# The down projection by products of seven as well, with its activation forms made in gate and up and passed through DRAM

## The chip, the cores and the metric

The kernel runs on one core of a Trainium2 chip. The metric is device time in microseconds (us); of the kernel before, three runs were timed, and the median stands for it. All details come from one more execution, taken by the hardware profiler. Names of engines: PE is the matrix engine (TensorE), DVE is VectorE, ACT is ScalarE, POOL is GpSimd, SP is the engine whose queue issues most transfers.

## The reference, cut to what matters

One block of a streaming encoder, on 512 positions (T) and 2048 channels (D): a norm, an input projection, two mixers, an output projection, and then the part that the change touches, a gated feed-forward net with 5632 inner channels (FF), a residual add and a last norm.

```python
def conv_ffn(h, w_gate, w_up, conv_w, conv_b, w_down):
    L = h.shape[1]
    a = h @ w_gate
    a_pad = jnp.pad(a, ((0, 0), (CONV_WIDTH - 1, 0), (0, 0)))
    a = sum(conv_w[j] * a_pad[:, j:j + L] for j in range(CONV_WIDTH)) + conv_b
    return (jax.nn.silu(a) * (h @ w_up)) @ w_down
...
    x = x + jnp.concatenate([o_a, o_b], axis=-1) @ w_out[l]
    h = rmsnorm(x, norm2_gain[l])
    x = x + conv_ffn(h, w_ffn_gate[l], w_ffn_up[l], ffn_conv_w[l], ffn_conv_b[l], w_ffn_down[l])
return rmsnorm(x, final_norm_gain)
```

Everything is float32. The kernel keeps that precision by splitting each operand of a product into a rounded part (hi) and a rest (lo), and by adding three matmuls: hi by hi, hi by lo, lo by hi.

## The kernel before

The program works on tiles of 128 channels by 512 positions. Stages, in the order of time: input projection, mixers and output projection (0 to 898 us); gate and up (904.7 to 1785.3 us); down (1787.9 to 2290.9 us), whose last rows are already the final norm.

**Gate and up by seven products.** For one row block f (128 of the 5632 inner channels, 44 blocks), gate and up are two outputs, and the positions are two halves of 256: a 2 by 2 block product, done with seven block products in place of eight. `glu(f)` asks for them one by one through `product` (L810). Product number i takes one weight combination, in the order `a11, s2, a12, s3, s1, a22, s4`, and one form of the activations, in the order of `NAMES`: `b11, n2, b21, t3, n1, n4, b22`. A form is a hi and a lo tile of 128 by 256 for each of 8 pairs of input blocks, so a product is 8 x 3 = 24 matmuls of 256 columns (L819 to L821), and a row block 168. `prepare` (L789) runs two products ahead (`LEAD`): ACT makes `fhi` (L807), DVE `flo` (L808) from a weight tile `wq` of 128 by 1024; four of each (pool `wh`) exist at a time. The weights come from DRAM by SP (L763); s1 and s3 are sums that a second, accumulating transfer from POOL makes (L765), s2 and s4 are DVE sums (L783). Eight tiles `wq` exist (pool `wf`). After its products, `glu` forms the gated value `uu` (L838 to L858), splits it into `ah` and `al` (L860, L861) and stores both in DRAM (`actd`, L863).

**Down by plain products.** The 44 blocks stand in four groups of 11 (`GF`, `NG`). For each of 16 output blocks d of 128 channels, one group is 11 x 3 = 33 matmuls of 512 columns, added to the residual tile `x1[d]` (L900). The activations come back from `actd`, issued by POOL (`acts_of`, L886); the weights come in pieces `raw` (L142) and are split by ACT (L149) and DVE (L150). In the last group, 12 output blocks are done like that, and the last four (`late`) with positions on the output's rows: 4 x 33 matmuls (L983 to L985), between which the final norm runs (`norm`, L955 to L975; `gained`, L948, scales 12 blocks by 4 quarters on ACT).

**What sets the order.** A scheduler writes one fixed order for each engine, from its own estimates of times; each engine runs its list in order, and a transfer waits on its queue's engine for its source and for a free target.

Of the kernel before, what the change touches and what calls it, by code (L numbers as in the profile page):

```python
# [8 lines left out]
F32 = mybir.dt.float32  # L9
# [13 lines left out]
GF = 11  # L23
NG = NF // GF
# [12 lines left out]
NPIECE_D = NF * KT * P // PIECE  # L37
QH = T // 2
KP = KT // 2
FORM = KP * P  # L40
LEAD = 2
DMA_SUMS = True
# [11 lines left out]
def tile_hymba_block(ctx: ExitStack, tc: tile.TileContext, xT, wst, wgu, wdn, wfb, consts, out, out_t):  # L54
# [10 lines left out]
    def closed(*names):  # L65
        for name in names:
            pools.pop(name)[0].__exit__(None, None, None)
# [28 lines left out]
    def f32(ap):  # L96
        return ap.bitcast(F32)
# [569 lines left out]
    actd = dr.tile([NF, 2, P, T], F32, name="actd")  # L667
# [18 lines left out]
    forms = {n: [] for n in NAMES}  # L686
    acc2 = tt.tile([P, T], F32, name="acc2")

    def form(name, j, src):
        pool = tt if j < KP - 1 else tl  # L690
        hi = pool.tile([P, QH], F32R, name=f"{name}h{j}")
        lo = pool.tile([P, QH], F32R, name=f"{name}l{j}")
        s.activation(hi, src, AF.Copy)
        v.tensor_tensor(lo, src, f32(hi), op=ALU.subtract)
        forms[name].append((hi, lo))

    def pair_forms(j, ha, hb):
        b11, b12, b21, b22 = ha[:, 0:QH], ha[:, QH:T], hb[:, 0:QH], hb[:, QH:T]

        def temp():  # L700
            return xr.tile([P, QH], F32, name="tq", tag="tq", bufs=2)

        form("b11", j, b11)
# [3 lines left out]
        form("n1", j, n1)  # L707
        form("n2", j, n2)
        form("b21", j, b21)
        v.tensor_tensor(n2, n2, b21, op=ALU.add)  # L710
        form("n4", j, n2)
        t3 = temp()
        v.tensor_tensor(t3, b22, b12, op=ALU.subtract)
        form("t3", j, t3)
        form("b22", j, b22)
# [25 lines left out]
    closed("xr")  # L741
    R2 = cp.tile([P, T], F32, name="R2", tag="R")
    nR2 = tl.tile([P, T], F32, name="nR2")
# [12 lines left out]
    raw = {}  # L756

    def W():
        return wf.tile([P, FORM], F32, name="wq", tag="wq")

    def load(f, name, q, q2=None):
        t = raw[f, name] = W()
        nc.sync.dma_start(out=t, in_=wgu[f, q])  # L763
        if q2 is not None:
            gp.dma_start(out=t, in_=wgu[f, q2], accum_op=ALU.add)  # L765

    def loads(f):

        if DMA_SUMS:
            load(f, "s1", 0, 1)  # L770
            load(f, "a11", 2)
            load(f, "s3", 0, 2)
            load(f, "a12", 3)
            load(f, "a22", 1)
        else:
            load(f, "a21", 0)
            load(f, "a22", 1)
            load(f, "a11", 2)
            load(f, "a12", 3)

    def add(f, name, x, y, into=None):
        t = raw[f, name] = W() if into is None else into
        v.tensor_tensor(t, raw[f, x], raw[f, y], op=ALU.add)  # L783

    def sums(f):
        if not DMA_SUMS:
            add(f, "s1", "a21", "a22")
            add(f, "s3", "a21", "a11", raw[f, "a21"])
        add(f, "s2", "s1", "a11")  # L789

    ready = {}

    def prepare(g):
        f, i = divmod(g, 7)
        if f >= NF:
            return
        if i == 0:
            sums(f)
            if f + 1 < NF:
                loads(f + 1)  # L800
        name = ORDER[i]
        if name == "s2":
            add(f, "s4", "s2", "a12")
        t = raw.pop((f, name))
        hi = wh.tile([P, FORM], F32R, name="fhi", tag="fhi")
        lo = wh.tile([P, FORM], F32R, name="flo", tag="flo")
        s.activation(hi, t, AF.Copy)  # L807
        v.tensor_tensor(lo, t, f32(hi), op=ALU.subtract)  # L808
        ready[g] = (hi, lo)

    def product(g, ps, first=True):
        prepare(g + LEAD)
        hi, lo = ready.pop(g)
        rhs = forms[NAMES[g % 7]]
        for j in range(KP):
            a, b = hi[:, j * P:(j + 1) * P], lo[:, j * P:(j + 1) * P]
            th, tl = rhs[j]
            kw = {"skip_group_check": not first}
            pe.matmul(ps, lhsT=a, rhs=th, start=(first and j == 0), stop=False, **kw)  # L819
            pe.matmul(ps, lhsT=a, rhs=tl, start=False, stop=False, **kw)  # L820
            pe.matmul(ps, lhsT=b, rhs=th, start=False, stop=(j == KP - 1), **kw)  # L821
            step()
# [4 lines left out]
    def G(name, shape=(P, T), dt=F32):  # L827
        return gt.tile(list(shape), dt, name=name, tag=name)

    def glu(f):  # L830
        cw = con[:, C_CW + 3 * f:C_CW + 3 * f + 3]
        g = 7 * f
        L, H = slice(0, QH), slice(QH, T)
        x, y, z, w = half(mm), half(mx), half(mm), half(mx)
        p1, u2, u3 = (G(n, (P, QH)) for n in ("p1", "u2", "u3"))
        a, uu = G("a"), G("uu")
        product(g, x)
        s.activation(p1, x, AF.Copy)  # L838
        product(g + 1, y)
        v.tensor_tensor(u2, p1, y, op=ALU.add)  # L840
        product(g + 2, x, first=False)
        s.activation(a[:, L], x, AF.Copy)
        product(g + 3, y, first=False)
        v.tensor_tensor(u3, p1, y, op=ALU.add)
        product(g + 4, z)
        v.tensor_tensor(uu[:, H], u3, z, op=ALU.add)
        product(g + 5, w)
        v.tensor_tensor(uu[:, L], u3, w, op=ALU.subtract)
        product(g + 6, z, first=False)
# [9 lines left out]
        hi, lo = G("ah", dt=F32R), G("al", dt=F32R)  # L859
        s.activation(hi, uu, AF.Copy)  # L860
        v.tensor_tensor(lo, uu, f32(hi), op=ALU.subtract)  # L861
        for i, part in enumerate((hi, lo)):
            nc.sync.dma_start(out=actd[f, i], in_=f32(part))  # L863

    loads(0)
    for g in range(LEAD):
        prepare(g)
    for f in range(NF):
        glu(f)
    closed("gt", "wh", "wf", "tl", "tt")  # L870


    wr = opened("wr", 3)
    wp = opened("wp", 4)
    pq = opened("pq", 81, "right")
# [5 lines left out]
    A = X = O  # L881

    def acts_of(f):
        parts = (O(F32R), O(F32R))
        for i, part in enumerate(parts):
            gp.dma_start(out=f32(part), in_=actd[f, i])  # L886
        return parts

    acts = [acts_of(f) for f in range(GF)]
    x1 = []  # L890
    for d in range(KT):
        t = X()
        gp.dma_start(out=t, in_=x1d[d])
        x1.append(t)
    for g in range(NG - 1):
        nxt = []
        for d in range(KT):
            ps = MX()
            unit(ps, range(GF), acts)
            v.tensor_tensor(x1[d], x1[d], ps, op=ALU.add)  # L900
            if d < GF:
                nxt.append(acts_of((g + 1) * GF + d))
        acts = nxt
# [22 lines left out]
    for d in range(ND):  # L926
        ps = MX()
        unit(ps, range(GF), acts)
        v.tensor_tensor(x1[d], x1[d], ps, op=ALU.add)
        square_acc(acc3, x1[d], d == 0)  # L930
        if d == ND - 2:
            ws.pool = O
    late = [ws.four() for _ in range(GF)]
    part = sm.tile([P, 4], F32, name="part")

    def sums3():
        yield 5
# [40 lines left out]
    for i in range(4):  # L978
        ys = gained(i)
        ps = MX()  # L980
        for k, (hi, lo) in enumerate(late):
# [3 lines left out]
            pe.matmul(ps, lhsT=xh, rhs=lo, start=False, stop=(k == GF - 1))  # L985
# [3 lines left out]
    closed("pq", "wp", "wr", "dr", "mx", "mm", "sm", "cp")  # L989


def _weights(w_in, w_out, w_gate, w_up, w_down):
# [22 lines left out]
    for g in range(NG):  # L1015
        rows = w_down[g * GF * P:(g + 1) * GF * P]
        nd = KT if g + 1 < NG else ND
        parts += [cols(rows, d * P, P) for d in range(nd)]
        parts += [cols(rows, nd * P, D - nd * P)] if nd < KT else []
# [8 lines left out]
    return rows_of(head), np.ascontiguousarray(wgu.reshape(NF, 4, P, FORM)), rows_of(parts)  # L1028
# [34 lines left out]
```

## Time and profile before

| what | us |
|---|---|
| median of 3 timed runs | 2302.2 |
| lowest and highest | 2300.54, 2302.64 |
| the profiled execution, its own time | 2302.55 |
| its span, first to last instruction | 2300.8 |
| PE busy in the span | 2273.4 |
| DVE, ACT, POOL busy | 1464.9, 939.2, 171.6 |

The times in the rows below count from the start of the span. A row of busy time gives the engine, how long it worked and in how many instructions; a timeline row gives start and duration of an instruction, and in brackets how long its engine had been idle and what ended that. "PEclk" is the granted clock of the PE as a share of full speed.

### The profile page before, as it was taken

To read this page: it belongs to the slowest core of one execution; us is meant where nothing else is said; L and a number is where in the kernel's file an instruction comes from. 1 tells how busy PE (TensorE), PEld (TensorE's weight loads), DVE (VectorE), ACT (ScalarE), POOL (GpSimd) and SP (SyncE) were. 2 spreads that over 40 slices of the span, in tenths; PEclk is the share of its full clock that TensorE was granted. 3 is DMA by queue.
4 is the path that set the end of the run, shared out by engine and by line. 5 is a ranking of instruction groups with operands and counts; after the bars stand their busy time and mean duration, and the time that the engine had idled before them with its cause. 6 is when DMAs were issued, how large, how long until landed. Compare 5 with 4: busy or idle time off the path is not lost.

```text
span 2300.8 us, 34411 instructions
## 1 busy us (share of the span) xinstructions
PE 2273.4 (99%) x13662; PEld 2012.7 (87%) x13662; DVE 1464.9 (64%) x2194; ACT 939.2 (41%) x1484; POOL 171.6 (7%) x259
## 2 busy tenths in 40 slices
PE   8999999999999998999999999999999999999998
PEld 7888888788888887999999999999999788888886
DVE  6666467556457565888888888888887333333345
ACT  5333233334335454544444554454444222222234
POOL 4000000000000000000000000000000512000000
PEclk9999999999999999999999999999999999999999
DMA  5222322222222455877877887878784955223223
GB/s 177 83 83 83 100 74 96 74 83 80 86 83 74 142 163 177 226 212 207 216 215 214 212 212 209 216 200 222 208 217 136 375 198 196 92 97 99 85 100 110
DMA packets 112210, 352.67 MB, mean 153 GB/s; under 512 B 12816, under 2 KB 19088, under 8 KB 112048
## 3 DMA queue, kind: packets, MB, share of 16 engines
q1 hardware_dynamic: 89568, 272.67, 36.0%
q0 software_dynamic: 22336, 77.67, 15.4%
q8 instruction: 107, 1.75, 0.3%
q14 instruction: 55, 0.45, 0.1%
q10 hardware_dynamic: 144, 0.12, 0.0%
HBM read 318.96 MB, written 31.46 MB: 152 GB/s over the span
## 4 chain that ended last, share of the span: by engine, by line
PE 95%; DMA 2%; DVE 1%; issue 1%; ACT 0%; POOL 0%; DVEq 0%; ACTq 0%; POOLq 0%
PE pq L819 12%; PE pq L820 12%; PE pq L821 12%; PE mmt L201 9%; PE mmt L203 9%; PE mmt L202 9%; PE mxt L202 7%; PE mxt L201 7%; PE mxt L203 7%; PE mmt L286 2%; PE mmt L284 2%; PE mmt L285 2%; DMA ot<-actd 1%; DMA wq<-wgu 1%; DMA raw<-wdn 1%
## 5 line engine op out<-in xcount | busy, mean ns | idle before, releaser
L150 DVE TENSOR_TENSOR wlo<-raw,whi 128x512 fp32r<-128x512 f32 x453 | 316.3, 699 | 464.5 <-ACT whi L149 424.9
L149 ACT ACTIVATE whi<-raw 128x512 fp32r<-128x512 f32 x453 | 284.8, 630 | 686.3 <-PE mxt L202 322.2
L807 ACT ACTIVATE fhi<-wq 128x1024 fp32r<-128x1024 f32 x308 | 326.6, 1061 | 365.7 <-PE pq L820 323.0
L808 DVE TENSOR_TENSOR flo<-wq,fhi 128x1024 fp32r<-128x1024 f32 x308 | 376.3, 1222 | 58.2 <-ACT fhi L807 52.4
L201 PE MATMUL mmt<-at,whi 128*128 128x512 f32 x896 | 354.8, 396 | 0.0
L203 PE MATMUL mmt<-at,wlo 128*128 128x512 f32 x896 | 349.8, 390 | 0.0
L202 PE MATMUL mmt<-at,whi 128*128 128x512 f32 x896 | 349.3, 390 | 0.0
L201 PE MATMUL mxt<-ot,whi 128*128 128x512 f32 x660 | 262.2, 399 | 2.9 <-ACT whi L149 2.7
L202 PE MATMUL mxt<-ot,whi 128*128 128x512 f32 x660 | 261.8, 397 | 0.5 <-DMA ot<-actd 0.5
L203 PE MATMUL mxt<-ot,wlo 128*128 128x512 f32 x660 | 261.6, 397 | 0.5 <-DVE wlo L150 0.5
L203 PEld LDWEIGHTS mmt<-at,wlo 128*128 128x128 f32 x896 | 168.2, 188 | 35.9
L201 PEld LDWEIGHTS mmt<-at,whi 128*128 128x128 f32 x896 | 168.3, 188 | 34.9 <-issue 1.9
L202 PEld LDWEIGHTS mmt<-at,whi 128*128 128x128 f32 x896 | 168.4, 188 | 33.1
L201 PEld LDWEIGHTS mxt<-ot,whi 128*128 128x128 f32 x660 | 124.5, 189 | 34.8 <-ACT whi L149 2.9
L202 PEld LDWEIGHTS mxt<-ot,whi 128*128 128x128 f32 x660 | 124.6, 189 | 31.8 <-DMA ot<-actd 2.1
L203 PEld LDWEIGHTS mxt<-ot,wlo 128*128 128x128 f32 x660 | 124.7, 189 | 30.6 <-DVE wlo L150 1.0
L765 POOL DMA_DIRECT2D wq<-wgu x88 | 75.9, 862 | 782.1 <-DVE flo L808 388.1
L783 DVE TENSOR_TENSOR wq<-wq 128x1024 f32<-128x1024 f32 x88 | 107.5, 1222 | 3.5 <-DMA wq<-wgu 2.0
L286 PE MATMUL mmt<-wlo,at 128*128 128x512 f32 x256 | 100.6, 394 | 4.4 <-DVE wlo L150 4.4
L819 PE MATMUL pq<-b11h,fhi 128*128 128x256 f32 x352 | 100.2, 285 | 3.6 <-ACT fhi L807 3.6
L284 PE MATMUL mmt<-whi,at 128*128 128x512 f32 x256 | 101.7, 397 | 0.3 <-ACT whi L149 0.3
L821 PE MATMUL pq<-b11h,flo 128*128 128x256 f32 x352 | 99.9, 284 | 1.3 <-DVE flo L808 1.3
(303 smaller groups left out, 5067.7 us busy)
## 6 DMA issues: line engine op xcount, KB each, us to landing
wq<-wgu SPq DMA_DIRECT2D x220, 512.0 KB, 4.5
raw<-wst SPq DMA_DIRECT2D x143, 512.0 KB, 3.5
wq<-wgu POOLq DMA_DIRECT2D x88, 512.0 KB, 7.3
raw<-wdn SPq DMA_DIRECT2D x87, 512.0 KB, 3.5
ot<-actd POOLq DMA_DIRECT2D x88, 256.0 KB, 6.6
actd<-ah SPq DMA_DIRECT2D x44, 256.0 KB, 3.2
actd<-al SPq DMA_DIRECT2D x44, 256.0 KB, 3.0
xt<-xT SPq DMA_DIRECT2D x16, 256.0 KB, 5.3
```

The source lines that it names most:

```text
L149: s.activation(hi, src, AF.Copy)
L150: v.tensor_tensor(lo, src, f32(hi), op=ALU.subtract)
L201: pe.matmul(ps, lhsT=a, rhs=xh[:, ts], start=(first and i == 0), stop=False)
L202: pe.matmul(ps, lhsT=a, rhs=xl[:, ts], start=False, stop=False)
L203: pe.matmul(ps, lhsT=b, rhs=xh[:, ts], start=False, stop=(last and i == n - 1))
L284: pe.matmul(pss[i], lhsT=xh[:, ts], rhs=hi, start=(k == 0), stop=False)
L286: pe.matmul(pss[i], lhsT=xh[:, ts], rhs=lo, start=False, stop=(k == KT - 1))
L807: s.activation(hi, t, AF.Copy)
L808: v.tensor_tensor(lo, t, f32(hi), op=ALU.subtract)
L819: pe.matmul(ps, lhsT=a, rhs=th, start=(first and j == 0), stop=False, **kw)
L820: pe.matmul(ps, lhsT=a, rhs=tl, start=False, stop=False, **kw)
L821: pe.matmul(ps, lhsT=b, rhs=th, start=False, stop=(j == KP - 1), **kw)
```

## The change

Of the 44 row blocks of the down projection, 40 become 20 pairs, and two output blocks d are done together: again a 2 by 2 block product (two inner blocks by two output blocks, halves of 256 positions) with seven products. Three chunks of 7, 7 and 6 pairs; in each chunk 8 units (two output blocks each); a unit has 7 products of n x 3 matmuls of 256 columns, n being 7 or 6. The other four row blocks (`FL`) stay as they were, with the late blocks and the final norm.

The code of `prepare` and `product` becomes a class `Seven` with one list of units, 44 of gate and up and then 24 of down, so that the weights of the next unit are loaded and split while the last one runs, through one ring of weight tiles (`wf`, now 7 in place of 8). s1 and s3 of a down unit are DVE sums, and s2 and s4 are now both made before the first product of a unit.

The forms of the down projection (seven per pair, hi and lo) are made in `glu` from two values `uu` of neighbouring blocks: four more DVE operations, seven ACT and seven DVE splits of 128 by 256, and 14 stores of 128 KB each per pair into `formd` (DRAM). At the start of a chunk, 98 (84) loads of 128 KB bring them back, on SP, into the tiles that held the forms before (`T7`: 14 tiles a name, one chunk). The residual tiles come in the first chunk, on POOL.

```diff
-    wf = opened("wf", 8)
-    wh = opened("wh", LEAD + 2)
+    wf = opened("wf", 7, "right")
+    wh = opened("wh", LEAD + 2, "right")
...
+    def T7(name):
+        return tt.tile([P, QH], F32R, name=name, tag=name, bufs=BUFS)
...
+            if i == 0:
+                if u == 0:
+                    self.loads(0)
+                if not self.units[u][2]:
+                    self.sum(u, "s1", "a21", "a22")
+                    self.sum(u, "s3", "a21", "a11", into="a21")
+                self.sum(u, "s2", "s1", "a11")
+                self.sum(u, "s4", "s2", "a12")
+                if u + 1 < len(self.units):
+                    self.loads(u + 1)
...
+        if f >= 2 * NPAIR:
+            hi, lo = G("ah", dt=F32R), G("al", dt=F32R)
...
+        def put(name, src):
+            hi, lo = G("of", (P, QH), F32R, bufs=6), G("of", (P, QH), F32R, bufs=6)
+            s.activation(hi, src, AF.Copy)
+            v.tensor_tensor(lo, src, f32(hi), op=ALU.subtract)
+            for i, part in enumerate((hi, lo)):
+                nc.sync.dma_start(out=formd[NAMES.index(name), f // 2, i], in_=f32(part))
+
+        seven(halves(*uus), lambda: G("tq", (P, QH), bufs=2), put)
...
+    for c, n in enumerate(CHUNKS):
+        dforms = {}
+        for i, name in enumerate(NAMES):
+            dforms[name] = []
+            for p in range(at, at + n):
+                parts = (T7(name), T7(name))
+                for k, part in enumerate(parts):
+                    nc.sync.dma_start(out=f32(part), in_=formd[i, p, k])
+                dforms[name].append(parts)
+        at += n
+        for m in range(KP):
+            if c == 0:
+                for d in (2 * m, 2 * m + 1):
+                    x1.append(xp.tile([P, T], F32, name=f"x1_{d}"))
+                    gp.dma_start(out=x1[d], in_=x1d[d])
...
+            sv.product(x, dforms)
+            s.activation(p1, x, AF.Copy)
+            sv.product(y, dforms)
+            v.tensor_tensor(u2, p1, y, op=ALU.add)
+            v.tensor_tensor(xe[:, H], xe[:, H], u2, op=ALU.add)
...
+    closed("gt", "wh", "wf", "tt")
...
-    acts = [acts_of(f) for f in range(GF)]
...
+    for f in range(FL):
+        acts.append((O(F32R), O(F32R)))
+        for i, part in enumerate(acts[-1]):
+            nc.sync.dma_start(out=f32(part), in_=actd[f, i])
...
-    late = [ws.four() for _ in range(GF)]
+    late = [ws.four() for _ in range(FL)]
```

The order on SP's queue where gate and up end and down begins, before: the stores of the last blocks, and the weights `raw` of down.

```order
L863 DMA actd_5863<-ah_18031 128x512
L863 DMA actd_5863<-al_18032 128x512
L142 DMA raw_18346<-wdn 128x512 x2
L142 DMA raw_18357<-wdn 128x1024
L142 DMA raw_18391<-wdn 128x1024
L142 DMA raw_18431<-wdn 128x1024
L863 DMA actd_5863<-ah_18249 128x512
L863 DMA actd_5863<-al_18250 128x512
L142 DMA raw_18471<-wdn 128x1024
```

The same place now: the loads of forms of chunk 0 (28 of 98 stand ahead of this piece, `b11` and `n2`), the last weight load `wq` of the second down unit, and the stores of the last gate and up block; 62 further loads of forms stand behind the last store, and behind them the weights of the third down unit.

```order
L936 DMA b21_19091<-formd_5864 128x256
L792 DMA wq_18953<-wd7 128x896
L936 DMA b21_19092<-formd_5864 128x256
...
L936 DMA b21_19103<-formd_5864 128x256
L904 DMA actd_5863<-ah_19021 128x512
L936 DMA b21_19104<-formd_5864 128x256
L904 DMA actd_5863<-al_19022 128x512
L936 DMA b21_19107<-formd_5864 128x256
```

What moved: the activations, which POOL's queue brought back, are now on SP's queue, in one row with the stores and the weights, each held up by the one ahead.

The order on PE at the first products of down, before: from the last matmul of gate and up straight into the first two output blocks (`mxt_18345`, `mxt_18411`), by activations `ot` and weights `whi`, `wlo`.

```order
L821 MATMUL pq_18039<-b22h7_7565,flo_18163 128x256
L201 MATMUL mxt_18345<-ot_18269,whi_18349 128x512
L202 MATMUL mxt_18345<-ot_18270,whi_18349 128x512
L203 MATMUL mxt_18345<-ot_18269,wlo_18350 128x512
L201 MATMUL mxt_18345<-ot_18273,whi_18349 128x512
L201 MATMUL mxt_18411<-ot_18269,whi_18359 128x512
```

Now, late in the first down unit (output `pq_19237`, its last form `b22`), the second unit (outputs `pq_19445` and `pq_19446`, forms `b21` and `t3`) is woven in.

```order
L850 MATMUL pq_19445<-b21_19112,fhi_19452 128x256
L851 MATMUL pq_19445<-b21_19111,flo_19453 128x256
L849 MATMUL pq_19445<-b21_19115,fhi_19452 128x256
L850 MATMUL pq_19445<-b21_19116,fhi_19452 128x256
L850 MATMUL pq_19237<-b22_19204,fhi_19348 128x256
L851 MATMUL pq_19237<-b22_19203,flo_19349 128x256
L851 MATMUL pq_19445<-b21_19115,flo_19453 128x256
L849 MATMUL pq_19446<-t3_19119,fhi_19478 128x256
L849 MATMUL pq_19237<-b22_19207,fhi_19348 128x256
```

What moved: the plain products are gone from this place, and where the first unit takes its last form, 241 of the two units' 294 matmuls stand ahead of its last one; 53 are left.

The order on DVE inside gate and up, at the start of a unit's weights, before: `flo` is the rest of a weight tile, `al` that of the gated value, and the two sums stand together.

```order
L858 TENSOR_TENSOR uu<-uu,t 128x512
L840 TENSOR_TENSOR u_12730<-p_12729,pq 128x256
L808 TENSOR_TENSOR flo<-wq,fhi 128x1024
L861 TENSOR_TENSOR al<-uu,ah 128x512
L783 TENSOR_TENSOR wq<-wq 128x1024 x2
L808 TENSOR_TENSOR flo<-wq,fhi 128x1024
L844 TENSOR_TENSOR u_12731<-p_12729,pq 128x256
```

The same place now, in every second block (in the other ones it holds three operations of the forms in place of eight): `of` and `tq` belong to the forms of down.

```order
L833 TENSOR_TENSOR flo<-wq,fhi 128x1024
L913 TENSOR_TENSOR of<-tq,of 128x256
L812 TENSOR_TENSOR wq<-wq 128x1024
L913 TENSOR_TENSOR of<-uu,of 128x256
L702 TENSOR_TENSOR tq<-tq,uu 128x256
L833 TENSOR_TENSOR flo<-wq,fhi 128x1024
L913 TENSOR_TENSOR of<-tq,of 128x256
L812 TENSOR_TENSOR wq<-wq 128x1024
L913 TENSOR_TENSOR of<-tq,of 128x256
L884 TENSOR_TENSOR u_13381<-p_13379,pq 128x256
L913 TENSOR_TENSOR of<-uu,of 128x256
```

What moved: the one operation `al` went, and 11 smaller ones per pair of blocks stand between the splits of the weights and the sums.

## Rows read from the trace of the kernel before

**Rows 1.** First part of the page: busy time, share, instructions of each engine.

```profile
PE 2273.4 (99%) x13662; PEld 2012.7 (87%) x13662; DVE 1464.9 (64%) x2194; ACT 939.2 (41%) x1484; POOL 171.6 (7%) x259
```

**Rows 2.** Windows: stretch and length, PE, PEld, DVE, ACT, POOL busy, PEclk, DMA share, GB/s.

```profile
915.00:1767.00 852.00, 852.00 (x7201) 852.00 (x7201) 715.36 (x858) 428.23 (x518) 73.27 (x85) 1.00 0.79 211
1785.00:1788.00 3.00, 0.33 (x4) 0.13 (x2) 1.72 (x3) 1.45 (x3) 2.54 (x5) 1.00 0.95 337
1788.00:1796.00 8.00, 7.49 (x19) 5.18 (x20) 4.60 (x8) 2.71 (x5) 5.43 (x11) 0.57 0.96 312
1796.00:1915.00 119.00, 118.34 (x502) 93.44 (x501) 38.56 (x58) 27.18 (x43) 39.44 (x74) 1.00 0.71 261
```

**Rows 3.** Timeline of DVE in one gate and up block: start, duration, instruction, [idle].

```profile
1379.75 0.41 DVE L844 TENSOR_TENSOR u<-p,pq 128x256 f32<-128x256 f32 x1
1380.15 1.22 DVE L808 TENSOR_TENSOR flo<-wq,fhi 128x1024 fp32r<-128x1024 f32 x1
1382.02 0.42 DVE L846 TENSOR_TENSOR uu<-u,pq 128x256 f32<-128x256 f32 x1 [0.64 <-PE pq L821]
1383.04 1.23 DVE L808 TENSOR_TENSOR flo<-wq,fhi 128x1024 fp32r<-128x1024 f32 x1 [0.60 <-ACT fhi L807]
...
1395.50 0.68 DVE L861 TENSOR_TENSOR al<-uu,ah 128x512 fp32r<-128x512 f32 x1
1396.10 2.48 DVE L783 TENSOR_TENSOR wq<-wq 128x1024 f32<-128x1024 f32 x2
...
1399.63 0.41 DVE L844 TENSOR_TENSOR u<-p,pq 128x256 f32<-128x256 f32 x1
```

**Rows 4.** Timeline of DVE in down, two residual adds, 33 matmuls apart.

```profile
2132.93 0.69 DVE L900 TENSOR_TENSOR ot<-ot,mxt 128x512 f32<-128x512 f32 x1 [1.67 <-PE mxt L203]
...
2140.63 0.69 DVE L900 TENSOR_TENSOR ot<-ot,mxt 128x512 f32<-128x512 f32 x1 [0.98 <-PE mxt L203]
```

**Rows 5.** Issues of transfers on the page: KB each, median us to landing.

```profile
wq<-wgu SPq DMA_DIRECT2D x220, 512.0 KB, 4.5
...
wq<-wgu POOLq DMA_DIRECT2D x88, 512.0 KB, 7.3
raw<-wdn SPq DMA_DIRECT2D x87, 512.0 KB, 3.5
...
actd<-al SPq DMA_DIRECT2D x44, 256.0 KB, 3.0
```

**Rows 6.** Timeline of two windows of DVE and PE: the last form, the first matmul of down.

```profile
903.79 0.42 DVE L694 TENSOR_TENSOR t3l<-tq,t3h 128x256 fp32r<-128x256 f32 x1
...
1787.94 0.50 PE L201 MATMUL mxt<-ot,whi 128*128 128x512 f32 x1 [2.67 <-ACT whi L149]
```

**Rows 7.** The chain of waits around the start of gate and up: start, length, what.

```profile
899.49 9.21 DMA wq<-wgu
908.73 1.23 DVE wq L783
```

**Rows 8.** SP's queue early in the program: issues of 256 KB transfers in a row.

```profile
2.19 1.85 SPq L270 DMA_DIRECT2D xt<-xT  x4
...
1779.61 0.81 SPq L142 DMA_DIRECT2D raw<-wdn  x2
```

**Rows 9.** Line L863, the stores of activations: issues with first and last start; us to landing.

```profile
L863 SPq DMA_DIRECT2D actd<-al x44: 319/327/327, 939.3 to 1792.2; - x44
...
DMA to landing us min/median/max: 2.0/3.1/8.4
```

**Rows 10.** Windows, as rows 2, while activations and residuals come in.

```profile
1805.00:1815.00 10.00, 9.78 (x43) 7.53 (x42) 4.57 (x7) 2.56 (x5) 5.46 (x12) 1.00 1.03 392
```

**Rows 11.** The end: first late matmul on PE, ACT's group L948, last chain.

```profile
2258.16 0.40 PE L983 MATMUL mxt<-ot 128*128 128x512 f32 x1
...
L948 ACT ACTIVATE ot<-ot,con 128x128 f32<-128x128 f32 x48 | 14.8, 387 | 0.0
...
2290.53 0.39 PE L985 MATMUL mxt<-ot 128*128 128x512 f32 x1
...
2291.74 0.63 ACT L958 ACTIVATE ot<-ot 128x512 f32<-128x512 f32 x1 [3.40 <-DVE ot L955]
```

More of the change, by code (lines that the diff above doesn't have):

```diff
@@ L685, in tile_hymba_block, with seven @@
     NAMES = ("b11", "n2", "b21", "t3", "n1", "n4", "b22")
[L686 to L703, printed above, removed]
+    BUFS = 2 * max(CHUNKS)
+    acc2 = tt.tile([P, T], F32, name="acc2", tag="acc")
+    def T7(name):
+        return tt.tile([P, QH], F32R, name=name, tag=name, bufs=BUFS)
+    def seven(b, temp, put):
+        (b11, b12), (b21, b22) = b
+        put("b11", b11)
         n1, n2 = temp(), temp()
@@ L781, in add @@
[L781 to L817, printed above, removed]
-            kw = {"skip_group_check": not first}
[L819 to L822, printed above, removed]
+    L, H = slice(0, QH), slice(QH, T)
@@ new lines, in tile_hymba_block, with __init__, add, tile @@
+    class Seven:
+        def __init__(self):
+            self.units = []
+            self.raw = {}
+            self.ready = {}
+            self.at = 0
+        def add(self, src, n, dma_sums):
+            self.units.append((src, n, dma_sums))
+        def tile(self, u, name):
+            t = self.raw[u, name] = wf.tile([P, self.units[u][1] * P], F32, name="wq", tag="wq")
+            return t
+        def loads(self, u):
+            src, n, dma_sums = self.units[u]
+            def load(name, q, q2=None):
+                t = self.tile(u, name)
+                nc.sync.dma_start(out=t, in_=src[q])
+                if q2 is not None:
+                    gp.dma_start(out=t, in_=src[q2], accum_op=ALU.add)
+            if dma_sums:
+                load("s1", 0, 1)
+                load("a11", 2)
+                load("s3", 0, 2)
+                load("a12", 3)
+                load("a22", 1)
+            else:
+                for q, name in enumerate(("a21", "a22", "a11", "a12")):
+                    load(name, q)
+        def sum(self, u, name, x, y, into=None):
+            if into is None:
+                t = self.tile(u, name)
+            else:
+                t = self.raw[u, name] = self.raw.pop((u, into))
+            x, y = (t if n == into else self.raw[u, n] for n in (x, y))
+            v.tensor_tensor(t, x, y, op=ALU.add)
+        def prepare(self, g):
+            u, i = divmod(g, 7)
+            if u >= len(self.units):
+                return
+            if i == 0:
[8 more added lines that the diff above has]
+                    self.loads(u + 1)
+            t = self.raw.pop((u, ORDER[i]))
+            n = self.units[u][1] * P
+            hi = wh.tile([P, n], F32R, name="fhi", tag="fhi")
+            lo = wh.tile([P, n], F32R, name="flo", tag="flo")
+            s.activation(hi, t, AF.Copy)
+            v.tensor_tensor(lo, t, f32(hi), op=ALU.subtract)
+            self.ready[g] = (hi, lo)
+        def product(self, ps, forms, first=True):
+            g = self.at
+            self.at += 1
+            for x in range(g + LEAD + 1):
+                if x >= g and x not in self.ready:
+                    self.prepare(x)
+            hi, lo = self.ready.pop(g)
+            rhs = forms[NAMES[g % 7]]
+            n = self.units[g // 7][1]
+            kw = {"skip_group_check": not first}
+            for j in range(n):
+                a, b = hi[:, j * P:(j + 1) * P], lo[:, j * P:(j + 1) * P]
+                th, tl_ = rhs[j]
+                pe.matmul(ps, lhsT=a, rhs=th, start=(first and j == 0), stop=False, **kw)
+                pe.matmul(ps, lhsT=a, rhs=tl_, start=False, stop=False, **kw)
+                pe.matmul(ps, lhsT=b, rhs=th, start=False, stop=(j == n - 1), **kw)
+                step()
@@ L858, in glu @@
         v.tensor_tensor(uu, uu, t, op=ALU.mult)
[L859 to L867, printed above, removed]
+        if f >= 2 * NPAIR:
+            hi, lo = G("ah", dt=F32R), G("al", dt=F32R)
+            s.activation(hi, uu, AF.Copy)
+            v.tensor_tensor(lo, uu, f32(hi), op=ALU.subtract)
+            for i, part in enumerate((hi, lo)):
+                nc.sync.dma_start(out=actd[f - 2 * NPAIR, i], in_=f32(part))
+            return
@@ L879, in O @@
         return pq.tile(list(shape), dt, name="ot", tag="q")
[L881 to L887, printed above, removed]
-    acts = [acts_of(f) for f in range(GF)]
[L890 to L903, printed above, removed]
+    A = O
+    acts = []
+    for f in range(FL):
+        acts.append((O(F32R), O(F32R)))
+        for i, part in enumerate(acts[-1]):
+            nc.sync.dma_start(out=f32(part), in_=actd[f, i])
     x1t, g3 = [], O()
@@ L1014, in _weights @@
     head, parts = parts, []
[L1015 to L1019, printed above, removed]
+    rows = w_down[2 * NPAIR * P:]
+    parts += [cols(rows, d * P, P) for d in range(ND)]
+    parts += [cols(rows, ND * P, D - ND * P)]
     def rows_of(parts):
```

146 lines of the change are left out of this document (88 added, 58 removed).

## The prediction, made before the changed kernel had run

> **What bounds the kernel now.** I read the shares of busy time first, then the windows by stage, then the cadence inside the two stages that the change touches, then the ends of these stages. PE is busy for 99% of the span [rows 1], and without a gap where it matters: 852.00 of 852 us in gate and up, 118.34 of 119 in the first part of down, both at full granted clock [rows 2]. DVE and ACT work beside it. So the time is a number of matmuls by their cadence, plus the few gaps at the seams. The cadence in gate and up: the same DVE operation comes at 1379.75 and again at 1399.63 [rows 3], 19.88 us for one block of 168 matmuls of 256 columns, 0.1183 us each. In down two residual adds stand 7.70 us apart [rows 4], 33 matmuls of 512 columns, 0.2333 us each.
>
> **The change part by part.** The base is the profiled span, 2300.8 us; 1.75 us lie around it (2302.55 less 2300.8), and the median of the three runs is 0.35 us lower than that execution.
>
> *Matmuls.* Gone are 40 blocks x 16 outputs x 3 = 1920 matmuls of 512 columns, 447.9 us. New are 20 pairs x 8 units x 7 products x 3 = 3360 of 256 columns, 397.5 us. That is 50.4 us less, all of it on PE, which sets the end. (Seven eighths of 447.9 would be 391.9; the narrower form gives 5.6 back.)
>
> *Start of gate and up.* The weight ring now lies over tiles that the last form frees, at 903.79 + 0.42 [rows 6], so the load of a11 begins there: 4.5 us [rows 5], then a rounding and a split, first product near 911. Before, the second product had to wait anyway for the accumulated s1 and its sum, which ended at 908.73 + 1.23 [rows 7], and for its own split, to about 912.4. So only the first product (2.84 us, or twice that at half clock) comes late: a loss of 2 to 6 us; I take 4.5.
>
> *Gate and up itself.* DVE is busy 715.36 of 852 us [rows 2], 33.4 us per pair of blocks out of 39.76. Two splits `al` of 0.68 go [rows 3], eleven operations of 128 x 256 come, at the 0.42 of such a split [rows 6]: 36.6 us, 92%. What hides them is DVE's idle time, in pieces of 0.6 us that end with a product's end on PE or with ACT's rounding [rows 3]; a DVE that runs late finds both done, and four tiles of `fhi` and `flo` let it be late by two or three products of 2.84 us. ACT is at half load, and SP's 14 stores per pair in place of four cost some 3 us of issue more out of 39.76. The other cover is the load of s1: it now waits for the split of the previous a11 (ends at 1381.4) and is wanted by the sum at 1396.10 [rows 3], 14.7 us; load, POOL's issue and accumulate take 4.5 + 0.9 + 7.3 = 12.7 [rows 5] (the 0.9 is an estimate, POOL's 73.27 us for 85 issues [rows 2]). Between 0 and 2 us remain. I cost the stage at nothing; every microsecond that is missing would come on each of 40 blocks (a rival, below).
>
> *Old seam to down.* It goes: 2.67 us of waiting [rows 6], 3.4 at low clock (8 us at 0.57 [rows 2]), 0.5 and 0.7 us of small waits: 7.3 us.
>
> *New seams: loads of forms.* This is the term that decides. There is room for one chunk of forms only, so most loads come when the old chunk is done, in a row on SP. No row shows transfers of 128 KB. Bounds for the pace: 0.33 us by bandwidth if 392 GB/s [rows 10] held, and also by SP's issue of 0.327 [rows 9]; above, four transfers of 256 KB in 1.85 us, 0.46 each, and two issues of 512 KB in 0.81 [rows 8]. SP's transfers go round eight completion counters, so the pace is never under an eighth of the landing time: 3.0 us of a 256 KB store gives 0.38, 4.5 of a weight load 0.56 [rows 5]. I take 0.43, next to the 256 KB row.
> Chunk 0, counted from the last matmul of gate and up (1785.27, from rows 6): SP comes past the last store at +6.9 (1792.2 [rows 9]); 62 loads are left: 6.9 + 62 x 0.43 + 2.2 to land (2.0 is the shortest store [rows 9]) = 35.8. PE has by then done 241 of the 294 matmuls of two units, which need 34.8 us without a wait; 53 x 0.1183 = 6.3 are left. Loss 35.8 + 6.3 - 34.8 = 7.3. The third unit's weights stand behind the forms on SP: 1.5 more. Sixteen residual tiles of 256 KB come over the same DMA engines, ten of them in this time, 6.7 us at 392 GB/s; as the forms leave a part of the bandwidth free I count 3. Together 12.
> Chunk 1: SP is held for 2.4 us by a weight tile whose split needs the last product; 71 loads are left: 2.4 + 30.5 + 2.2 = 35.1, loss 6.6, with the weights behind 8.1. Chunk 2 (84 loads, 56 left; 45 of 252 matmuls left): 2.3 + 24.1 + 2.2 + 5.3 - 29.8 = 4.1, with the weights 5.6. In sum 25.7 us; each 0.01 us of pace is worth 189 loads, 1.9 us.
>
> *Down itself.* A unit of 7 pairs lasts 147 x 0.1183 = 17.4 us; DVE has eleven operations of 7/8 of 1.22 us and some 3.3 us of adds, 15 us. Four weight loads of 448 KB per unit ask about 103 GB/s. Both are hidden.
>
> *Seam to the last four blocks.* The weights `raw` wait for tiles that the very last of the new matmuls frees: issue 0.3, load 3.5 [rows 5], rounding and split 1.3, about 5.2 us of idle PE, and after that a low clock as at the old seam, 3.4. I take 9 (6 to 10).
>
> *Tail.* From the first late matmul (2258.16 [rows 11]) to the end it is 42.6 us; 84 of its matmuls go, 19.6 us (counted above). But PE then no longer covers ACT: 48 scalings take 14.8 us, a square, its read-out and a root about 1.0 per quarter, 2.0 for the first sum and the table load, and 2300.8 - 2291.74 = 9.1 us lie behind the last square [rows 11]: 29.5 where PE alone would give 23.0. Loss 6.5 (4 to 8).
>
> *Sum.* 2300.8 - 50.4 + 4.5 - 7.3 + 25.7 + 9 + 6.5 = 2288.8; with 1.75 around it, and 0.35 to the median, **2290 us**. The gain is gone where the seams of the forms cost 37.7 in place of 25.7 us, that is at a pace of 0.49.
>
> **A rule weighed against this.** The rows show 392 GB/s with transfers of 256 and 512 KB, several in flight [rows 10]. The Trainium skill, in "DMA: Bandwidth & Descriptors", section "Bandwidth", asks for transfers of 1 MiB or more, and gives 341 GB/s for 1 MB and 138 GB/s for 64 KB. That speaks against loads of 128 KB; at 138 GB/s one would take 0.95 us, and the time would be an estimated 2290 + 189 x 0.52 = 2388 us. By that rule transfers of 512 KB would not reach 392 GB/s either, so the trace does not agree with it where several overlap.
>
> **The rivals.**
> 1. *Loads of forms paced by their landing* (slower). If a 128 KB load lands in 4.5 us, as weight loads do, eight in flight give 0.56 a load: 25.7 + 189 x 0.13 = 50.3 us of seams, 2315 us. It decides from 0.52 on, where the kernel is 0.2% slower. For it: the row of 256 KB at 0.46 is not far. Against: stores land in 3.0. Chance 0.18; a still slower pace, with a time above 2340, has 0.03 of it.
> 2. *DVE or the load of s1 becomes the bound of gate and up* (slower). If three quarters of DVE's 6.4 us of idle per pair stayed, 36.6 + 4.8 = 41.4 in place of 39.76: 33 us over 20 pairs, 2323 us. It decides from half of the idle time on. One microsecond too late for s1 in each block gives 40. Against: idle pieces follow PE, and PE has products in store. Chance 0.12.
> 3. *Seams nearly hidden.* At 0.36 a load and with residuals out of the way, the forms cost 12 us: 2277 us. For it: 392 GB/s and 0.327 of issue. Chance 0.20.
> 4. *Low clock in each chunk.* Where PE waits in pieces for forms, the clock may fall as at the old seam [rows 2]; three times 3.4 us, unless it waits anyway, gives 2300 us: no change that can be told. Chance 0.15.
>
> **How the numbers follow.** My forecast has the remaining 0.35. Its own range is 2282 to 2298 (pace 0.40 to 0.46 with the ends of the small terms). The wanted range takes in rival 3 with the small terms at their low ends (2, 6 and 4 us: 2269) and most of rivals 1 and 2, up to 2330. A measurement of this kernel can tell about 0.2% from no change, 4.6 us. Faster by more: 0.33 of the forecast's 0.35, 0.20, and a third of rival 4, 0.58. Within: 0.02, 0.08 of rival 4 and 0.03 of rivals 1 and 2, 0.13. Slower: 0.29.
>
> **What would show it.** Gate and up with PE at 100% and 19.88 us a block says that DVE and s1's load are hidden; more than that is rival 2. At the seams the issues of forms on SP give the pace, and PE's idle time there should be near 12, 8 and 6 us; the granted clock there judges rival 4. A gap of about 5 us must stand ahead of the last four blocks, and ACT must be without a break in the tail. The forecast is wrong if the pace lies beyond 0.36 to 0.49, or if PE waits inside gate and up.

## The result, and the profile after

The changed kernel takes 2342.8 us (median; 2341.8 to 2343.8), the kernel before 2302.4 in the same comparison: the ratio is 1.0177, with an interval of 1.0159 to 1.0195. It is 40 us slower, where 12 us less were forecast. The profiled span grew from 2300.8 to 2340.1 us.

The first part of the page after (busy time, share, instructions; before in [rows 1]):

```profile
PE 2274.1 (97%) x15102; PEld 2087.3 (89%) x15102; DVE 1701.5 (73%) x2622; ACT 1017.5 (43%) x1616; POOL 125.0 (5%) x171
```

PE's busy time did not fall, although 50 us of matmuls were to go. The windows tell where it went (stretch and length, PE, PEld, DVE, ACT, POOL busy, PEclk, DMA share, GB/s), first gate and up, which answers to [rows 2], then the start of chunks 0 and 1 of down:

```profile
915.00:1767.00 852.00, 844.77 (x7013) 842.01 (x7014) 736.52 (x1012) 437.20 (x605) 72.73 (x85) 1.00 0.83 227
...
1812.00:1822.00 10.00, 6.99 (x47) 5.96 (x45) 6.16 (x8) 3.96 (x5) 2.15 (x4) 0.88 1.05 384
1822.00:1832.00 10.00, 5.72 (x16) 4.00 (x16) 4.55 (x6) 1.13 (x3) 3.18 (x6) 0.50 1.06 367
1832.00:1842.00 10.00, 7.99 (x28) 6.72 (x28) 3.35 (x5) 1.90 (x2) 0.00 (x0) 0.50 0.91 289
1842.00:1852.00 10.00, 9.17 (x53) 8.49 (x54) 3.62 (x5) 2.06 (x3) 0.00 (x0) 0.76 0.83 254
1852.00:1862.00 10.00, 10.00 (x86) 10.00 (x85) 4.95 (x8) 2.86 (x3) 0.00 (x0) 1.00 0.90 263
...
1986.00:1996.00 10.00, 9.28 (x32) 7.13 (x31) 4.38 (x5) 0.95 (x1) 0.00 (x0) 0.54 0.88 265
```

In gate and up PE has 7013 matmuls in the stretch that held 7201 before, at full clock; it is 2.7% slower there, and two thirds of the missing time is not idle time at all (7.2 us are). In chunk 0, PE makes 47, 16, 28 and 53 matmuls in ten microseconds where 84 are the full pace.

To sort the time I take the starts of the products' matmuls from the trace: when a unit of gate and up begins, when a chunk of down begins, when the last product ends. Cadence is the time from the start of one matmul to the start of the next where nothing waits; a seam is what PE loses where one stage or chunk gives way to the next. (A chunk's loss is its length less its matmuls at the cadence of gate and up.)

| term of the sum (profiled spans, us) | forecast | measured |
|---|---|---|
| stages before gate and up, unchanged code | 0 | +1.4 |
| start of gate and up (first product 913.6, before 904.7) | +4.5 | +7.2 |
| cadence in gate and up (a block 20.11, before 19.88) | 0 | +10.3 |
| further waits in gate and up | 0 | +8.6 |
| matmuls of down (3360 at 0.1197, less 447.9) | -50.4 | -45.7 |
| old seam | -7.3 | -7.3 |
| seams of the forms (chunks 23.4, 15.9, 11.3) | +25.7 | +50.6 |
| seam to the last four blocks, and tail | +15.5 | +15.4 |
| sum (the spans differ by 39.3) | -12.0 | +40.5 |

The measured rows add up to 1.2 us more than the spans differ: 0.2 of it is the cadence of the first block, which stands in the second row and the third, and the rest was not found. The old seam is the forecast's own reading of the kernel before.

The start, on the timelines of PE, SP and ACT of the kernel after:

```profile
913.61 0.58 PE L849 MATMUL pq<-b,fhi 128*128 128x256 f32 x1 [10.25 <-ACT fhi L832]
```

```profile
906.50 0.33 SPq L792 DMA_DIRECT2D wq<-wgu  x1
```

```profile
912.50 1.06 ACT L832 ACTIVATE fhi<-wq 128x1024 fp32r<-128x1024 f32 x1 [6.52 <-DMA wq<-wgu]
```

PE stands idle for 10.25 us, because the load of a11 now starts only after the last form, at 906.50, and lands 5.98 us later, at 912.48; then ACT rounds it.

### The profile page after: what moved, and what is told of

The parts are those of the page before. It is cut to its first block, busy times and chain, and to the rows that moved or that the text cites. A ratio compares the mean times of both kernels' runs of the same rounds, so it can differ in the third digit from the quotient of the medians.

```text
span 2340.1 us, 38889 instructions
## 1 busy us (share of the span) xinstructions
PE 2274.1 (97%) x15102; PEld 2087.3 (89%) x15102; DVE 1701.5 (73%) x2622; ACT 1017.5 (43%) x1616; POOL 125.0 (5%) x171
## 4 chain that ended last, share of the span: by engine, by line
PE 88%; DMA 6%; DVE 3%; issue 2%; ACT 1%; SPq 0%; DVEq 0%; POOLq 0%; ACTq 0%
PE pq L849 17%; PE pq L850 16%; PE pq L851 16%; PE mmt L200 9%; PE mmt L202 9%; PE mmt L201 9%; PE mmt L285 2%; PE mmt L283 2%; PE mmt L284 2%; DMA wq<-wgu 2%; DMA formd<-of 2%; PE mxt L200 1%; PE mxt L201 1%; DMA b<-formd 1%; PE mxt L202 1%
## 5 line engine op out<-in xcount | busy, mean ns | idle before, releaser
L832 ACT ACTIVATE fhi<-wq 128x1024 fp32r<-128x1024 f32 (+2 forms) x476 | 479.7, 1009 | 668.1 <-PE pq L850 626.4
L833 DVE TENSOR_TENSOR flo<-wq,fhi 128x1024 fp32r<-128x1024 f32 (+2 forms) x476 | 550.5, 1158 | 86.8 <-ACT fhi L832 86.8
L849 PE MATMUL pq<-b,fhi 128*128 128x256 f32 x1404 | 403.0, 287 | 21.5 <-ACT fhi L832 11.3
L850 PE MATMUL pq<-b,fhi 128*128 128x256 f32 x1404 | 402.9, 287 | 4.1 <-DMA b<-formd 4.1
L849 PE MATMUL pq<-n,fhi 128*128 128x256 f32 x1404 | 398.2, 285 | 3.6 <-DMA n<-formd 3.1
L851 PE MATMUL pq<-b,flo 128*128 128x256 f32 x1404 | 400.9, 286 | 0.5 <-DVE flo L833 0.5
L850 PE MATMUL pq<-n,fhi 128*128 128x256 f32 x1404 | 398.8, 285 | 2.2 <-DMA n<-formd 2.1
L851 PE MATMUL pq<-n,flo 128*128 128x256 f32 x1404 | 398.0, 284 | 1.7 <-DVE flo L833 1.7
L849 PEld LDWEIGHTS pq<-b,fhi 128*128 128x128 f32 x1404 | 272.6, 194 | 26.4 <-ACT fhi L832 14.9
L850 PEld LDWEIGHTS pq<-b,fhi 128*128 128x128 f32 x1404 | 272.1, 194 | 7.3 <-DMA b<-formd 6.8
L849 PEld LDWEIGHTS pq<-n,fhi 128*128 128x128 f32 x1404 | 270.4, 193 | 5.2 <-DMA n<-formd 3.8
L850 PEld LDWEIGHTS pq<-n,fhi 128*128 128x128 f32 x1404 | 269.9, 193 | 3.9 <-DMA n<-formd 3.5
L851 PEld LDWEIGHTS pq<-b,flo 128*128 128x128 f32 x1404 | 272.5, 194 | 0.9 <-DVE flo L833 0.8
L851 PEld LDWEIGHTS pq<-n,flo 128*128 128x128 f32 x1404 | 270.2, 193 | 2.4 <-DVE flo L833 2.4
```

Source lines behind the costliest of these rows:

```text
L850: pe.matmul(ps, lhsT=a, rhs=tl_, start=False, stop=False, **kw)
L851: pe.matmul(ps, lhsT=b, rhs=th, start=False, stop=(j == n - 1), **kw)
```

## The experiments

**Where the weight tiles lie.** The cadence was nobody's suspect. The three matmuls of each block are the same in both kernels, and so is the granted clock, but nearly all starts are 119 to 121 ns apart in the kernel after, where they swung between 112 and 122 before. What differs is the place of the tiles in on-chip memory (byte addresses of the built programs): `fhi` and `flo` begin at 4064 modulo 4096 in the kernel after, at 2400 before; of the 112 form tiles of gate and up 98 begin at 992 modulo 1024 in both, and 14, those of the last pair of input blocks, at 352. So modulo 1024 weights and most forms have the same place after (992), and different ones before (352). The first experiment moves `wh`, and nothing else, down by 640 bytes, to 352:

```diff
+    pad = opened("pad", 1, "right")
+    pad.tile([P, 160], F32, name="pad")
     wh = opened("wh", LEAD + 2, "right")
```

> One change: the four fhi and four flo tiles lie 640 bytes lower in on-chip memory (as they lay before, counted modulo 1024). Theory 'address': the matmuls of 256 columns take 0.1197 us in place of 0.1183 because weight tiles and forms now have the same place modulo 1024; with the shift the cadence goes back to 0.1183 in gate and up and in down, 10752 x 0.0014 = 15 us less, about 2328 us. Rival 'layout of the forms' (hi and lo of one name side by side in rings): the cadence stays at 0.1197 and the time at 2343.

Measured: 2328.0 us, ratio to the kernel before 1.0107 (1.0092 to 1.0122), that is 14.8 us less than the changed kernel; a block takes 19.88 us. The same pad ahead of `wh` in the kernel before brings its tiles to 992 (the temporaries of `glu`, which lie behind them, move along):

> The kernel before with its fhi and flo tiles moved by 640 bytes, to the place modulo 1024 that they have in the changed kernel. Theory 'address': its gate and up cadence rises from 0.1183 to about 0.1197, 7392 x 0.0014 = 10 us more, about 2312.5 us. Rival 'layout of the forms': nothing changes, 2302.4.

Measured: 2313.2 us, 1.0043 (1.0027 to 1.0060). One stretch of gate and up without any wait, first the kernel before, then the kernel before with the shift (columns as above):

```profile
1000.00:1700.00 700.00, 700.00 (x5918) 700.00 (x5917) 586.96 (x704) 349.92 (x422) 60.36 (x70) 1.00 0.80 213
```

```profile
1000.00:1700.00 700.00, 700.00 (x5849) 700.00 (x5848) 581.02 (x696) 344.78 (x417) 59.95 (x70) 1.00 0.77 210
```

PE is busy all the time in both, at full clock, and does 69 matmuls less in the second: 0.1183 and 0.1197 us each. So the place of the weight tiles sets the cadence, both ways; the layout of the forms in rings does not matter. Whether their own place counts or their place relative to the forms was not tried, as no run moves the forms. One thing speaks against the relative place: in the kernel before, the forms of the last pair begin at 352 like the weights, and its three matmuls of each product are not slow; the time from start to start is 116.1 ns for them and 118.6 for the other 21 (means over the trace). One run with 512 in place of 640 bytes asks which part of the address counts:

> The changed kernel with the split tiles of the weights moved by 512 in place of 640 bytes: another place modulo 1024 than that of the forms, the same place modulo 512. If only the place modulo 1024 counts, the cadence is 0.1183 us (a gate and up block 19.88 us); if the place modulo 512 or less counts, it stays at 0.1197 (20.11).

Measured: a block takes 20.11 us, 2339.9 us in a single run. So a move by 512 bytes, to 480 modulo 1024, leaves the slow cadence. Which smaller part counts, and what in the chip it is, stays open.

**The stores of the forms.** In gate and up the waits came in every second block only. A timeline of ACT and, below it, of DVE in the changed kernel shows one of them:

```profile
1132.49 0.42 ACT L912 ACTIVATE of<-tq 128x256 fp32r<-128x256 f32 x1 [0.58 <-DMA formd<-of]
...
1136.28 0.42 ACT L912 ACTIVATE of<-uu 128x256 fp32r<-128x256 f32 x1 [2.41 <-DMA formd<-of]
```

```profile
1137.57 0.42 DVE L913 TENSOR_TENSOR of<-uu,of 128x256 fp32r<-128x256 f32 x1 [2.83 <-DMA formd<-of]
```

```profile
1139.61 0.36 PE L849 MATMUL pq<-b,fhi 128*128 128x256 f32 x1 [1.07 <-ACT fhi L832]
```

ACT waits for the landing of a store, because it may write the next form only into a tile whose store has landed, and there are six; behind it in its queue stands the rounding `fhi`, for which PE then waits 1.07 us. Experiment: ten tiles `of`; `ah` and `al` of the last blocks use the tiles of `a` and `t`.

```diff
-            hi, lo = G("of", (P, QH), F32R, bufs=6), G("of", (P, QH), F32R, bufs=6)
+            hi, lo = G("of", (P, QH), F32R, bufs=10), G("of", (P, QH), F32R, bufs=10)
```

> One change: the ring of tiles for the forms of down has ten in place of six (the split of the last four blocks uses two other tiles). Theory 'stores': the waits of PE in gate and up, some 8 us over 44 blocks, come from ACT and DVE waiting in order for a store to land before they may write the next form (idle ended by formd<-of); with ten tiles they go, 2335 us or a little more. Rival 's1 and DVE': the waits come from a full DVE or from the load of s1; the ring changes nothing, 2343.

Measured: 2333.5 us, 1.0128 (1.0113 to 1.0143). The waits beyond the regular cadence fell from 8.6 to 0.06 us (with six tiles they were 4.8 to 12.0 us in the other runs that leave the stores as they are), and the window of the run shows PE without a gap, with DVE at 88%:

```profile
1000.00:1700.00 700.00, 700.00 (x5849) 700.00 (x5848) 618.48 (x858) 363.82 (x507) 59.47 (x69) 1.00 0.85 230
```

So neither DVE nor the load of s1 bounds gate and up.

**The seams of the forms.** The line of these loads in the kernel after (duration of the issue on SP in ns, min/median/max; us to landing):

```profile
L936 SPq DMA_DIRECT2D b<-formd x120: 319/382/1482, 1792.7 to 2164.3; - x120
...
DMA to landing us min/median/max: 2.1/3.4/8.0
```

and a piece of SP's timeline at the end of gate and up:

```profile
1815.85 0.33 SPq L792 DMA_DIRECT2D wq<-wd  x1
1816.88 4.29 SPq L936 DMA_DIRECT2D b<-formd  x6
1822.89 0.32 SPq L904 DMA_DIRECT2D actd<-ah  x1
1823.30 0.38 SPq L936 DMA_DIRECT2D b<-formd  x1
1824.10 0.32 SPq L904 DMA_DIRECT2D actd<-al  x1
1824.51 2.81 SPq L936 DMA_DIRECT2D b<-formd  x6
```

From 1824.51 on six loads take 2.81 us; the loads that nothing holds up start every 0.474 us. Is it the issue, the place in SP's queue, or the bytes? The first experiment on this changed two things at once: one tile and one transfer of 256 KB for both parts of a form, in stores and loads, and the loads issued by POOL.

```diff
+                both = T7(name)
+                gp.dma_start(out=f32(both), in_=formd[i, p])
```

> The hi and lo parts of a form lie in one tile and move in one transfer of 256 KB (7 stores per pair, 49 loads per chunk), and the loads of forms are issued by POOL, so that they do not stand behind stores and weights on SP and can start as each form's tiles come free. Theory 'issue': the seams cost 50 us because SP issues a 128 KB load every 0.474 us and is held for 2 to 12 us at the start of a chunk; at 392 GB/s a 256 KB load takes 0.67, and most loads start some 10 us earlier: seams of 10 to 20 us, 2305 to 2315 us. Rival 'bytes': the 12.8 MB of a chunk over the DMA engines set the pace whoever issues: seams stay above 40 us, 2335 or more.

Measured: 2336.7 us, 1.0141 (1.0126 to 1.0156). The seams fell from 50.6 to 30.7 us (12.5, 10.7, 7.5), but the waits in gate and up rose from 8.6 to 26: three double tiles are held by stores longer than six single ones (ACT waited 77.9 us for landings of these stores, 44.8 in the changed kernel). The time thus hid the gain. So I took the parts one by one, with the stores as they were. Only the loads merged, on SP:

> One change: the two parts of a form lie side by side and come back in one load of 256 KB, still on SP; the stores stay apart. Theory 'issue': SP issues every 0.474 us whatever the size, so 49 loads of 256 KB come at the pace of the DMA engines (395 GB/s in the run with both changes, 0.66 us each) in place of 98 at 0.474: 9 us less per chunk, seams from 51 to some 25 us, 2317 us. Rival 'place in the queue': what costs is that SP is held behind weights and stores; then merging saves under 3 us per chunk, 2333 or more.

Measured: 2319.6 us, 1.0074 (1.0060 to 1.0088), 23 us less than the changed kernel. The seams are 17.5, 6.6 and 6.2 us, together 30.3, 20 less; the other 3 or 4 are waits in gate and up, 4.8 in place of 8.6. Its windows at the start of chunk 1 show the DMA engines full, where the changed kernel had 0.88 and 265 GB/s from 1986 on:

```profile
1976.00:1986.00 10.00, 8.96 (x52) 6.73 (x53) 5.54 (x7) 1.90 (x2) 0.00 (x0) 1.00 1.02 381
1986.00:1996.00 10.00, 9.86 (x81) 9.54 (x81) 4.97 (x8) 3.87 (x5) 0.00 (x0) 1.00 1.05 389
```

Only the queue changed, with loads of 128 KB from POOL:

> One change: the 98 loads of 128 KB of a chunk are issued by POOL in place of SP. Theory 'issue': POOL issues one in 0.53 us (its pace with 256 KB in the run before), 52 us per chunk, less an earlier start by 10 to 14 us: seams about 40 to 50 us, 2332 to 2343 us, no great gain. Rival 'place in the queue': the loads start when tiles come free and the seams fall below 30 us, under 2323.

Measured: 2351.6 us, 1.0211 (1.0195 to 1.0227), slower still and above what was expected; seams 22.8, 23.6 and 14.8, together 61, and waits of 12.0 us in gate and up. POOL's timeline shows its pace, 17 loads in 9.01 us, 0.53 each:

```profile
1998.20 9.01 POOL L936 DMA_DIRECT2D n<-formd  x17
```

The loads start when a tile comes free, from 1961.49, 17 us before the chunk; but so did SP's in the changed kernel (from 1959.43), and POOL's end later, because POOL takes longer for each. So what sets the pace of loads of 128 KB in chunks 1 and 2 is the cost of an issue. It did not depend on the size: POOL took 0.53 us for 256 KB too, where nothing held it, and SP 0.46 [rows 8]. In chunk 0 the queue counts as well: with merged loads it cost 17.5 us by SP and 12.5 by POOL, where the residuals, which POOL loads too, share the queue with the forms. With merged loads the bytes become the limit.

Merging changed a second thing, which no run separates: the packets of these loads are of 2 KB in place of 1 KB. The windows give 265 GB/s at a share of 0.88 and 389 at 1.05, by estimate 301 and 370 for full engines. So without any cost of issue, loads of 128 KB would have come every 0.474 x 0.88 = 0.42 us at best (an estimate), 5.6 us less for the 98 of a chunk. Merged, they take some 13 us less (98 x 0.474 less 49 x 0.68), so more than half of that would be due to the larger packets.

Why chunk 0 costs more than the others was asked of the kernel with merged loads on SP:

> The run with merged loads on SP, but the sixteen residual tiles of 256 KB are set to zero by POOL in place of being loaded (so the residual is left out of the result). It asks why chunk 0 costs 17.5 us where chunks 1 and 2 cost 6.6 and 6.2. Theory 'bytes': residuals take their share of DMA engines that are already full (1.04 of their time): 4.2 MB at 390 GB/s are 10.7 us, of which those that come between the forms count: chunk 0 falls to 8 to 11 us. Rival 'held queue': SP waits for the stores of the last gate and up blocks before it may issue on: chunk 0 stays at 15 us or more.

Measured: chunk 0 fell from 17.5 to 9.3 us, near the 7.2 of chunk 1 (2313.8 us, ratio 1.0047, 1.0029 to 1.0065, though its gate and up lost 5 us more in waits). The residuals' 4.2 MB on full DMA engines cost 8 us; some 2 are left for the held queue.

**All together.** The pad, ten tiles, merged loads on POOL with separate stores:

> Weight tiles shifted by 640 bytes, ten tiles for the forms' stores, loads of 256 KB issued by POOL (stores stay two of 128 KB). If the four causes add: 2342.8 - 15 (cadence) - 9 (stores) - 20 (seams) = 2299 us, 0.2% below the kernel before. If the stores' waits come back, as with three double tiles in the run with both changes, 2310 or more; if earlier loads of forms disturb the weights of gate and up, 2305.

Measured: 2297.9 us, 0.9980 (0.9971 to 0.9989). The causes add, as 2299 was expected. Then the ring `wf` under `wh`, so that the first weights of gate and up lie over tiles that are free earlier:

```diff
+    pad = opened("pad", 1, "right")
+    pad.tile([P, 160], F32, name="pad")
-    wf = opened("wf", 7, "right")
     wh = opened("wh", LEAD + 2, "right")
+    wf = opened("wf", 7, "right")
```

> As the combined kernel, and the weight ring wf lies lower than the split tiles, so that the first weight loads of gate and up do not wait for the last form before it (an accumulated load of s1 and the load of a11 start some 4 to 6 us earlier). If the start costs what the trace says, 4 to 6 us less than the combined kernel, 2293 to 2295 us; if the start is set by DVE's forms and the norm, no change.

Measured: 2291.7 us, 0.9958 (0.9945 to 0.9970), 6 less; the first product starts again as early as in the kernel before:

```profile
904.67 0.58 PE L852 MATMUL pq<-b,fhi 128*128 128x256 f32 x1 [3.67 <-ACT fhi L835]
```

Last, POOL loads the forms of chunk 0 alone:

```diff
-                gp.dma_start(out=f32(both), in_=formd[i, p].rearrange("p k t -> p (k t)"))
+                (nc.sync if c else gp).dma_start(out=f32(both), in_=formd[i, p].rearrange("p k t -> p (k t)"))
```

> As the combined kernel with the swapped rings, but only chunk 0's forms are loaded by POOL, those of chunks 1 and 2 by SP. The seams of chunks 1 and 2 were 6.6 and 6.2 us in the run with merged loads on SP, against 9.8 and 6.3 here by POOL: about 3 us less, 2288 us. If the two runs' difference came from elsewhere (other addresses, other timing of the weights), no change, 2291.7.

Measured: 2286.1 us, 0.9925 (0.9912 to 0.9939), the fastest of all: 16 us under the kernel before. The seams of chunks 1 and 2 are 7.2 and 5.0 us, against 9.8 and 6.3, chunk 0 has 13.3. Another 2 us came behind the last product, where the swapped kernel took 76.6 us, this one 74.5 and the other runs 74 to 75; why the swapped one took longer was not followed. Its gate and up is at the old cadence, with DVE at 89%:

```profile
1000.00:1700.00 700.00, 700.00 (x5918) 700.00 (x5917) 624.50 (x865) 368.31 (x512) 60.37 (x70) 1.00 0.85 232
```

## Why the prediction was wrong

- **The sign.** The forecast and its first rival lay on the two sides of one number, a pace of 0.49 us per load. What pushed the result over the edge was not one term but four: seams +24.9, cadence +10.3 and +4.7 (0.1197 in place of 0.1183 for 10752 matmuls), waits for stores +8.6, start +2.7, each for the worse. The time lies above the stated range.
- **Matmuls.** The count was right; the step "3360 of 256 columns, 397.5 us" took the cadence of [rows 3] as a property of the matmul's shape. It belongs to the shape and the place of the weight tiles, which the change moved.
- **Gate and up at nothing.** Right for the two covers that I examined: DVE at 88% and the load of s1 did not hold PE. The step that failed is the list of covers. I counted the 14 stores per pair as issue time on SP, "some 3 us", and did not ask who waits for their landing. The row that could have told it was there: a store took 2.0 to 8.4 us to land [rows 9], and six tiles are filled in less than a block. An added store is an added wait for the next writer of its tile, and here that writer stands ahead of `fhi` in ACT's queue.
- **Start.** The mechanism was right, the size too small: the load of a11 began 2.3 us later than counted, at 906.50, since the last form came later (1.4 of that is the late end of the stages before), and it took 5.98 us, not the median 4.5 of [rows 5]; what held it was not tried, but with the ring elsewhere the first product came 6.9 us earlier (911.6 in the combined kernel, 904.7 in the swapped one).
- **Seams.** The sum says that a chunk loses (last load's landing) + (matmuls left) - (two units' work). In chunk 0 the last load landed at 1862.1, 49.7 us after the last product of gate and up (1812.4), where 35.8 were forecast; 49.7 + 6.3 - 35.2 = 20.8 of the measured 23.4. Chunks 1 and 2 give 13.6 of 15.9 and 10.1 of 11.3 in the same way, so the form of the sum holds for 44.5 of the 50.6 us. The other 6 are not the weights behind the forms, for which the forecast had 1.5 a chunk: when the last loads landed, 72, 70 and 53 matmuls were left in place of 53, 53 and 45, and from there on PE had no gap. They fit the low clock (rival 4).
  The size that was wrong is the time of the last landing. Of the 14 us in chunk 0, 4.8 are the last store (1824.10, +11.7 in place of +6.9), 2.7 the pace (0.474 in place of 0.43) and the rest waits while the DMA engines were full with residuals, for which 3 us were counted and which cost 8 in the run without them. The row of 256 KB issues, 0.46 each [rows 8], was the better one; I took it as an upper bound and went below it towards the bandwidth of [rows 10].
- **The rule weighed** there, that of the Trainium skill, "DMA: Bandwidth & Descriptors", section "Bandwidth", to batch transfers, held in its direction: 256 KB in place of 128 KB took 20 us off the seams. Its price did not: at the 138 GB/s that the Trainium skill gives there for 64 KB a load would have cost an estimated 0.95 us, and the run shows 0.474 with several in flight.
- **Rivals.** Rival 1 came nearest. In chunk 0 its mechanism was there: with the DMA engines full, loads took up to 8.0 us to land, and SP, whose transfers take eight completion counters in turn, stood for over 8 us until a transfer eight places ahead had landed (rows below: what SP waited for from 1812.4 to 1859.3, us in total, times, longest). The pace there was 0.566, waits included. In chunks 1 and 2 such waits were 1.5 and 0.9 us, and the issue set the pace. Rival 2 is refuted by the ring of ten tiles. Rival 4's low clock came, and longer than I thought: 0.50 from 1822 to 1842, 0.54 from 1986 to 1996. Most of it stands in time that the loads take anyway; the 6 us beyond the sum above are the most that it can have cost. What it costs alone was not tried.

```profile
SPq L936 <- DMA b<-formd: 3.5, 4, 1.5
SPq L936 <- DMA n<-formd: 1.9, 3, 0.7
...
SPq L792 <- DMA wq<-wd: 1.6, 1, 1.6
SPq L936 <- DMA wq<-wd: 1.1, 1, 1.1
```

- **Right as forecast:** the idle of about 5.2 us ahead of the last four blocks (5.23 in the row below), and a tail bound by ACT. That both together cost 15.4 us, forecast 15.5, is luck: from the first late matmul (2308.97) to the end it took 31.1 us, not 29.5 (a sum whose pieces, with four quarters of 1.0, give 29.9), so the tail lost 8.1 in place of 6.5, and that leaves 7.3 in place of 9 for the seam.

```profile
2271.15 0.80 PE L200 MATMUL mxt<-ot,whi 128*128 128x512 f32 x1 [5.23 <-ACT whi L148]
```

## What to carry to other kernels

A transfer has three prices: its issue on the engine that starts it, its time on the shared DMA engines, and the time in which its tile may not be written again; count all three for each new store and load, and merge small ones before looking for another queue (merging took 20 us off the seams here, the other queue added 10). A change that moves tiles can change the cadence of matmuls that it does not touch, so measure that cadence again before explaining a loss by waits. Here the idea itself was sound: with these losses made smaller, the kernel with the down projection by products of seven is 0.75% faster than the kernel before.

## What the runs showed of the hardware that was not expected

- The place of the weight tiles in on-chip memory sets the cadence of float32 matmuls with 256 columns: 0.1197 us when they begin at 992 or 480 modulo 1024, 0.1183 when they begin at 352, with nearly all moving tiles at 992; 10 us in the kernel before, 15 in the kernel after. Whether the place of the moving tile plays a part was not tried.
- SP starts a load of 128 KB every 0.474 us where nothing holds it, and POOL one every 0.53 us; loads of 256 KB on SP came every 0.68 us (median of their starts in chunk 1), with the DMA engines full at 381 to 389 GB/s.
- With packets of 1 KB the DMA engines moved 265 GB/s at a busy share of 0.88, with packets of 2 KB 389 GB/s at 1.05.
